# One transfer and one buffer for each 512 KB unit of weights in a decoder-layer kernel

## The chip, the cores and the metric

The kernel runs on one core of a Trainium2 chip. Its time is the device time of one launch in microseconds (us). TensorE (PE in the profile) does the matmuls, VectorE (DVE), ScalarE (ACT) and GpSimd (POOL) the rest, and SyncE (SP) issues nearly all transfers (DMAs) in the order of the program. Each of these engines works through its own list in order and waits at semaphores for the others. Sixteen DMA engines move the data.

## What is computed

One decoder layer in float32, for one sequence of 256 positions and 1024 channels. The reference, cut to its course:

```python
proj = x @ w_in                      # -> q | k | v | B | C | h | gate_attn | gate_conv
q, k = apply_partial_rope(q, cos, sin), apply_partial_rope(k, cos, sin)
y_att = moba_attention(q, k, v) @ w_attn_out
y_cnv = (gate_b * causal_dwconv(gate_c * h_in, conv_w_mix)) @ w_conv_out
mix = (g_att * y_att + g_cnv * y_cnv) @ w_o
x = layer_norm(DEEPNORM_ALPHA * x + mix, ln1_g, ln1_b)
u = causal_dwconv(x @ w_up, conv_w_ffn)
f = (silu(u[..., :D_FF]) * u[..., D_FF:]) @ w_down
x = layer_norm(DEEPNORM_ALPHA * x + f, ln2_g, ln2_b)
```

With 256 positions there is a single key block, so the attention is plain causal attention with 8 heads of 64. The feed-forward width is 2816.

## The kernel before

Every matmul is done with float32 operands that are split into a high part (cast to float32r) and a low part (the rest), and three products high x high, high x low and low x high are summed. So each weight that arrives must be split first: ACT casts the raw tile to the high part `wh` (lines 198 and 220), DVE subtracts it from the raw tile and gives the low part `wl` (lines 203 and 221). A *unit* is a piece of weights with 1024 float32 numbers in each of the 128 partitions, 512 KB. Six or twelve matmuls use it, and there are nine buffers for `wh` and nine for `wl`.

The host packs all weights into one array `wpack` in the order of their use, so a transfer is one contiguous read. `plan()` (line 73) lists the units and groups them in *chunks*. A chunk is one buffer and, with the exceptions in `PIECES` (line 52), one transfer. Most chunks hold two units: 2048 numbers, 8 KB in each partition, 1 MB. The first eight chunks hold one k-tile each of the product with q and k: 256 columns of the transposed x and one unit of weights, 5 KB in each partition. Chunk 0 is cut in three transfers and chunk 1 in two. `RAW_BUFS = 3` buffers of 8 KB take the chunks in turn.

`issue_dma(c)` (line 177) issues all chunks up to c on SP's queue. A transfer into a buffer that is still being read waits on SP until the split of the buffer's last unit is done, and SP's later transfers wait behind it. `split_start(u)` and `split_h(u)` (lines 189 and 194) call it for the chunk two after that of unit u, so a chunk's transfer is issued when the first unit of the chunk two before it is split.

The stages, in order of time:

- *q and k* (lines 595 to 618): for each of eight k-tiles, x's tile and the unit are split, and 12 matmuls of 512 columns follow. The splits of the first four v units stand among the last two k-tiles. After the last matmuls of q and of k, ACT evacuates them (`evac_rows`, line 556).
- *v, h, C, B and the gates* (lines 744 to 760): 16 units of 12 matmuls and 16 units of 16 matmuls. After each unit a *slot* (`mid_slot`, `step`, lines 527 and 740) emits the attention's and the convolution's tasks whose lag in slots is over, and `mid_ahead` (line 732) emits splits four to six units ahead of PE. Tasks that issue transfers are emitted before the slot's splits. Such are the exchanges that transpose through memory: rotated q and k are turned in blocks by DVE and written (`qk_write`, `qkd`), and three slots after that of the second write read back (`qk_read`, `qkl`); `qk_high` and `qk_low` then split them for the scores. The probabilities (`pd`, `sm`) and the convolution (`cvd`, `convl`) take the same way.
- *y, o and the first norm* (lines 786 to 856).
- *the feed-forward* (lines 968 to 1078): u and its convolution, with the exchange `ud`, `uts` through memory, the gated product and the down product; `slot(k)` splits four to seven units ahead of PE.

The pool `tmp` has six scratch buffers with the tag "scr", 2 KB in each partition, that hold small intermediate results in turn; in the q and k stage they are not in use.

Of the kernel before, what the change touches and what calls it, by code (L numbers as in the profile page):

```python
# [8 lines left out]
F32 = mybir.dt.float32  # L9
# [6 lines left out]
P = 128  # L16
S = 256
# [29 lines left out]
    return parts  # L47


CHUNK = 2048  # L50

PIECES = {0: (0, 256, 768, 1280), 1: (0, 768, 1280)}
OFF_V, OFF_B, OFF_C, OFF_H, OFF_G = 2 * AW, 3 * AW, 3 * AW + CW, 3 * AW + 2 * CW, 3 * AW + 3 * CW
TAIL = 8
GROUPS = NP // 2
# [17 lines left out]
def plan():  # L73


    chunks, units, first = [], [], {}

    def chunk(*us):
        c, off = len(chunks), 0
        chunks.append([])  # L80
        for k, n, blocks in us:
            chunks[c].append(len(units))
            units.append((c, off, k, n, blocks))
            off += k * n
        assert off <= CHUNK

    def mark(name):
        first[name] = len(units)

    def cols(w, c0):  # L90
        chunk(*[(8, P, [(w, 0, 8, c0 + u * P, c0 + (u + 1) * P)]) for u in range(2)])

    def rows(w, k):
        chunk(*[(1, D, [(w, k + u, k + u + 1, 0, D)]) for u in range(2)])


    mark("qk")
    for k in range(KT):
        chunk((1, S, [("xT", k, k + 1, 0, S)]), (2, 512, [("w_in", k, k + 1, 0, 1024)]))

    def wide(w, c0):
        for half in range(2):
            chunk(*[(2, 512, [(w, k, k + 2, c0, c0 + 512)]) for k in (4 * half, 4 * half + 2)])

    for off in (OFF_V, OFF_H, OFF_C, OFF_B):
        mark(off)
        wide("w_in", off)
    for pr in range(8):
        mark(("g", pr))
        cols("w_in", OFF_G + pr * 256)  # L110

    for half in range(2):
        for nm in ("ao", "co"):
            mark((nm, half))
            chunk(*[(4, 256, [(nm, 0, 4, half * 512 + u * 256, half * 512 + u * 256 + 256)]) for u in range(2)])
    mark("wo")
    for k in range(0, 8, 2):
        rows("w_o", k)

    for kind, c in [("u", 0)] + FFN_ORDER:  # L120
        mark((kind, c))
        if kind == "d":
            rows("w_dn", 2 * c)
            continue
        for half in range(2):
            chunk(*[(2, 512, [("w_up", k, k + 1, c0, c0 + 256)
                              for k in (4 * half + 2 * u, 4 * half + 2 * u + 1)
                              for c0 in (256 * c, DFF + 256 * c)]) for u in range(2)])
    return chunks, units, first
# [17 lines left out]
def layer_kernel(ctx: ExitStack, tc: tile.TileContext, x, wpack, cpack, ln1_g, ln1_b, ln2_g, ln2_b, out):  # L147
# [4 lines left out]
    wp = ctx.enter_context(tc.tile_pool(name="wp", bufs=1))  # L152
# [12 lines left out]
    def scratch(shape, name, bufs=None, tag="scr"):  # L165
        return tmp.tile(shape, F32, tag=tag, name=name, bufs=bufs or 6)

    RAW_BUFS, HL_BUFS, PR_BUFS = 3, 9, 4  # L170
    TURN = nc.sync
    chunks, plan_units, U = plan()
    blocks = transfers(chunks, plan_units)
    units = [dict(chunk=c, off=off, shape=(k, n), h=None, l=None) for c, off, k, n, _ in plan_units]
    raws = []

    def issue_dma(c):
        while len(raws) <= c and len(raws) < len(chunks):
            i = len(raws)
            t = wp.tile([P, CHUNK], F32, tag="raw", name=f"raw{i}", bufs=RAW_BUFS)  # L180
            raws.append(t)
            for a, b, off in blocks[i]:
                nc.sync.dma_start(t[:, a:b], wpack[off:off + P * (b - a)].rearrange("(p n) -> p n", p=P))

    def alloc(u, part, tag):
        k, n = units[u]["shape"]
        units[u][part] = wp.tile([P, k, n], F32R, tag=tag, name=f"{tag}{u}", bufs=HL_BUFS)

    def split_start(u):
        issue_dma(units[u]["chunk"] + RAW_BUFS - 1)  # L190
        alloc(u, "h", "wh")
        alloc(u, "l", "wl")

    def split_h(u):

        issue_dma(units[u]["chunk"] + RAW_BUFS - 1)
        alloc(u, "h", "wh")
        nc.scalar.activation(units[u]["h"], raw_of(u), AF.Copy)  # L198

# [19 lines left out]
    def hl_split(h, l, src, eng=None):  # L219
        nc.scalar.activation(h, src, AF.Copy)  # L220
        (eng or nc.vector).tensor_tensor(l, src, h.bitcast(F32), op=ALU.subtract)  # L221
# [5 lines left out]
    nc.gpsimd.memset(ident, 0.0)  # L227
    nc.gpsimd.affine_select(out=ident, in_=ident, compare_op=ALU.not_equal, fill=1.0, base=0,
                            pattern=[[-1, P]], channel_multiplier=1)
    issue_dma(1)  # L230
    warm = ps_bank("warm")

    def warm_up(n):
# [27 lines left out]
    xh, xl = xT[:, :, 0], xT[:, :, 1]  # L261
# [306 lines left out]


    def x_split(k):  # L570
        issue_dma(k + RAW_BUFS - 1)
        hl_split(xh[:, k, :], xl[:, k, :], raws[k][:, 0:S])

    def qk_split(k):
        if k < KT:
# [17 lines left out]


    split_start(1)
    issue_dma(RAW_BUFS - 1)
    nc.vector.tensor_copy(xh[:, 0, :], raws[0][:, 0:S])
    nc.vector.tensor_tensor(xl[:, 0, :], raws[0][:, 0:S], xh[:, 0, :].bitcast(F32), op=ALU.subtract)
    w0, wh0, wl0 = raw_of(1), units[1]["h"], units[1]["l"]
# [145 lines left out]
    for nm, off in (("v", OFF_V), ("h", OFF_H), ("c", OFF_C), ("b", OFF_B)):  # L745
        GB[nm] = [(ps_bank if nm == "v" else acc_bank)(f"{nm}{t}") for t in range(2)]
        for c in range(4):
            u = U[off] + c
# [4 lines left out]
    for j in range(16):  # L753
        u = U[("g", 0)] + j
# [6 lines left out]
    k = U[("ao", 0)] - C0  # L761
# [24 lines left out]
    for half in range(2):  # L786
        for e in range(2):
            ua, uc = U[("ao", half)] + e, U[("co", half)] + e
            for n in range(2):
                i = half * 4 + e * 2 + n  # L790
# [237 lines left out]
    for k, (kind, i, u) in enumerate(seq[:tail_from]):  # L1028
        if kind == "u":
            c, h = i  # L1030
# [56 lines left out]
def packed(inputs):  # L1087
# [6 lines left out]
    chunks, units, _ = plan()  # L1094
    rows = np.zeros((len(chunks), P, CHUNK), np.float32)
    for c, off, k, n, blocks in units:
# [27 lines left out]
```

## Time and profile before

| | us |
|---|---|
| three runs | 360.8, 361.29, 365.44 |
| median | 361.29 |
| profiled execution | 361.71 |
| its span (first to last instruction) | 359.9 |

Busy time in the span:

| engine | us | share |
|---|---|---|
| PE, matmuls | 348.8 | 97% |
| DVE | 298.3 | 83% |
| ACT | 208.5 | 58% |
| POOL | 64.6 | 18% |

The core moved 88.50 MB at 246 GB/s on average.

In the rows below, L with a number is the line of the kernel. A row of the timeline has the start of an instruction in us, its length, the engine, the line, the operation, the tile that it writes and, after the arrow, the tiles that it reads, then its size and how many like it were merged; in brackets stands how long the engine was idle just before, and what ended that. A row of the waits has who waited for whom, then us in total, times and the longest. `raw` is a chunk's buffer, `wpack` the packed weights, `wh` and `wl` a unit's parts, `xT` x's parts. Successive matmuls overlap, so a matmul's length is longer than the step from one to the next.

### The profile page before, as it was taken

The numbers are of one execution on the slowest core, as the hardware profiler recorded it, in microseconds if no ns is written. First come the engines' busy times: TensorE is split into PE (matmuls) and PEld (weight loads), VectorE is DVE, ScalarE is ACT, GpSimd is POOL, SyncE is SP. The second block draws the span as 40 slices with busy tenths as digits, with TensorE's granted clock in tenths as the row PEclk, the third lists the DMA queues.
The fourth block names the chain that finished last, engine by engine and source line by source line (L and its number), as shares of the span: only waits on it lengthen the run. The fifth ranks groups of instructions, "written<-read, shape, count | busy, mean of one in ns | idle before, by whom it ended". The sixth has DMA issues, their size and how long they took to land.

```text
span 359.9 us, 5040 instructions
## 1 busy us (share of the span) xinstructions
PE 348.8 (97%) x1762; PEld 294.5 (82%) x1762; DVE 298.3 (83%) x466; ACT 208.5 (58%) x346; POOL 64.6 (18%) x75
## 2 busy tenths in 40 slices
PE   8999999999999989999999999999999999999991
PEld 7787888888888979988888888888888888888891
DVE  4757939987899879869894999999899988798884
ACT  3659519769888955633362567756556745457200
POOL 2000000454442000102100221231130230230211
PEclk9999999999999999999999999999999999999997
DMA  7797788689995765496249999699969879856011
GB/s 255 274 308 279 295 229 300 227 291 322 273 320 171 300 237 201 180 345 239 112 176 335 280 298 312 233 291 334 305 224 294 289 232 323 252 192 188 0 60 58
DMA packets 33322, 88.50 MB, mean 246 GB/s; under 512 B 2704, under 2 KB 19472, under 8 KB 26000
## 3 DMA queue, kind: packets, MB, share of 16 engines
q1 hardware_dynamic: 32576, 85.88, 71.4%
q0 software_dynamic: 576, 2.10, 1.8%
q8 instruction: 14, 0.23, 0.3%
q10 hardware_dynamic: 144, 0.20, 0.2%
q14 instruction: 12, 0.10, 0.1%
HBM read 77.68 MB, written 10.49 MB: 245 GB/s over the span
## 4 chain that ended last, share of the span: by engine, by line
PE 83%; DMA 5%; DVE 5%; ACT 4%; issue 2%; POOL 1%; SPq 0%; DVEq 0%; ACTq 0%
PE up L309 11%; PE up L307 11%; PE up L308 11%; PE d L309 5%; PE d L308 5%; PE d L307 5%; DMA raw<-in_wpack 5%; PE g L336 5%; PE g L338 2%; PE o L309 2%; PE o L308 2%; PE o L307 2%; PE y L327 2%; PE y L328 2%; PE y L326 2%
## 5 line engine op out<-in xcount | busy, mean ns | idle before, releaser
L203 DVE TENSOR_TENSOR wl<-raw,wh 128x1024 fp32r<-128x1024 f32 x90 | 111.6, 1253 | 5.2 <-ACT wh L198 5.0
L198 ACT ACTIVATE wh<-raw 128x1024 fp32r<-128x1024 f32 x90 | 93.0, 1050 | 15.2 <-DMA raw<-in_wpack 14.7
L307 PE MATMUL up<-wh,x1T 128*128 128x512 f32 x176 | 68.6, 390 | 0.0
L309 PE MATMUL up<-wh,x1T 128*128 128x512 f32 x176 | 68.5, 389 | 0.0
L308 PE MATMUL up<-wl,x1T 128*128 128x512 f32 x176 | 68.5, 389 | 0.0
L923 POOL TENSOR_TENSOR ff<-fs,fc 128x256 f32<-128x256 f32 x22 | 30.3, 1378 | 131.3 <-DVE fc L914 128.5
L221 DVE TENSOR_TENSOR wl<-raw,wh 128x1024 fp32r<-128x1024 f32 (+1 forms) x34 | 37.9, 1141 | 7.8 <-ACT wh L220 7.6
L220 ACT ACTIVATE wh<-raw 128x1024 fp32r<-128x1024 f32 (+1 forms) x34 | 32.5, 987 | 13.0 <-DMA raw<-in_wpack 8.7
L309 PEld LDWEIGHTS up<-wh,x1T 128*128 128x128 f32 x176 | 33.0, 188 | 6.9
L308 PEld LDWEIGHTS up<-wl,x1T 128*128 128x128 f32 x176 | 33.0, 188 | 6.9
L307 PEld LDWEIGHTS up<-wh,x1T 128*128 128x128 f32 x176 | 33.0, 188 | 6.7
L336 PE MATMUL g<-xT,wh 128*128 128x512 f32 x128 | 32.0, 392 | 0.0
L926 ACT ACTIVATE f<-ff 128x256 fp32r<-128x256 f32 x22 | 9.2, 420 | 38.3 <-POOL ff L923 38.3
L307 PE MATMUL d<-wh,f 128*128 128x512 f32 x80 | 31.1, 389 | 0.0
L308 PE MATMUL d<-wl,f 128*128 128x512 f32 x80 | 31.1, 389 | 0.0
L309 PE MATMUL d<-wh,f 128*128 128x512 f32 x80 | 31.1, 389 | 0.0
L456 POOL TENSOR_SCALAR sm<-sm,st 128x128 f32<-128x128 f32 (+1 forms) x16 | 17.5, 1107 | 74.3 <-ACT wh L198 65.6
L912 DVE SCALAR_TENSOR_TENSOR second<-uts,consts,tap 128x256 f32<-128x256 f32 x44 | 23.7, 539 | 6.6 <-ACT tap L905 4.7
L905 ACT ACTIVATE tap<-uts,consts 128x256 f32<-128x256 f32 x44 | 20.3, 500 | 14.6 <-DMA uts<-ud 14.2
L336 PEld LDWEIGHTS g<-xT,wh 128*128 128x128 f32 x128 | 23.1, 188 | 4.3
L914 DVE SCALAR_TENSOR_TENSOR fc<-uts,consts,second 128x256 f32<-128x256 f32 x44 | 23.4, 533 | 1.6
L362 DVE STREAM_TRANSPOSE stg<-up 128x512 f32<-128x512 f32 x22 | 14.5, 695 | 8.8 <-PE up L309 8.8
(180 smaller groups left out, 632.9 us busy)
## 6 DMA issues: line engine op xcount, KB each, us to landing
raw<-in_wpack SPq DMA_DIRECT2D x57, 1024.0 KB, 6.1
ud<-stg SPq DMA_DIRECT2D x11, 512.0 KB, 4.0
uts<-ud SPq DMA_DIRECT2D x44, 128.0 KB, 5.5
raw<-in_wpack SPq DMA_DIRECT2D x6, 640.0 KB, 4.9
pd<-ps SPq DMA_DIRECT2D x4, 384.0 KB, 5.8
sm<-pd SPq DMA_DIRECT2D x16, 96.0 KB, 4.4
qkd<-qks SPq DMA_DIRECT2D x2, 512.0 KB, 3.4
qkl<-qkd SPq DMA_DIRECT2D x4, 256.0 KB, 4.6
```

The source lines that it names most:

```text
L198: nc.scalar.activation(units[u]["h"], raw_of(u), AF.Copy)
L203: nc.vector.tensor_tensor(units[u]["l"], raw_of(u), units[u]["h"].bitcast(F32), op=ALU.subtract)
L220: nc.scalar.activation(h, src, AF.Copy)
L221: (eng or nc.vector).tensor_tensor(l, src, h.bitcast(F32), op=ALU.subtract)
L307: nc.tensor.matmul(o, ah, bh, start=start, stop=False)
L308: nc.tensor.matmul(o, ah, bl, start=False, stop=False)
L309: nc.tensor.matmul(o, al, bh, start=False, stop=stop)
L336: nc.tensor.matmul(bank, un["h"][:, k, :], b[:, k].rearrange("p a s -> p (a s)"), start=k == 0, stop=False)
L905: nc.scalar.activation(rows_of(taps[i % 2][:, a, 1:S + 1]), unit_of(i, a), AF.Copy, scale=w_ffn(0, j))
L912: nc.vector.scalar_tensor_tensor(rows_of(sec[:, 1:S + 1]), unit_of(i, a), w_ffn(1, j), rows_of(first[:, 0:S]), op0=ALU.mult, op1=ALU.add)
L914: nc.vector.scalar_tensor_tensor(rows_of(FF["c", i][:, a]), unit_of(i, a), w_ffn(2, j), rows_of(sec[:, 0:S]), op0=ALU.mult, op1=ALU.add)
L923: nc.gpsimd.tensor_tensor(FF["f", i], FF.pop(("s", i)), FF.pop(("c", i))[:, 1], op=ALU.mult)
```

## The change

A chunk holds one unit. `CHUNK` goes from 2048 to 1024 numbers in each partition and `RAW_BUFS` from 3 to 6, so that the buffers have 24 KB in each partition as before, and each unit has a transfer of 512 KB with rows of 4 KB. The eight k-tiles of x become chunks of their own (128 KB, rows of 1 KB) and land in the scratch buffers "scr" in place of the raw buffers; unit 2k is x's k-tile k and unit 2k + 1 the weights that go with it. The first two weight units are cut in two transfers each.

`order_for(u)` replaces the direct call of `issue_dma`: it issues up to unit u + 5; while q and k are loaded, where every second unit is one of x, up to unit u + 10, at most 15, the last of that stage. The first call issues four units (two k-tiles) in place of two chunks (the same data), and the split of unit 1 then issues up to unit 11, the sixth k-tile.

```diff
-CHUNK = 2048
-
-PIECES = {0: (0, 256, 768, 1280), 1: (0, 768, 1280)}
+CHUNK = 1024
+
+PIECES = {1: (0, 512, 1024), 3: (0, 512, 1024)}
...
     def chunk(*us):
-        c, off = len(chunks), 0
-        chunks.append([])
         for k, n, blocks in us:
-            chunks[c].append(len(units))
-            units.append((c, off, k, n, blocks))
-            off += k * n
-        assert off <= CHUNK
+            assert k * n in (S, CHUNK)
+            chunks.append([len(units)])
+            units.append((len(units), 0, k, n, blocks))
...
-    RAW_BUFS, HL_BUFS, PR_BUFS = 3, 9, 4
+    RAW_BUFS, HL_BUFS, PR_BUFS = 6, 9, 4
...
             i = len(raws)
-            t = wp.tile([P, CHUNK], F32, tag="raw", name=f"raw{i}", bufs=RAW_BUFS)
+            if i < U[OFF_V] and i % 2 == 0:
+                t = scratch([P, S], f"x{i // 2}")
+            else:
+                t = wp.tile([P, CHUNK], F32, tag="raw", name=f"raw{i}", bufs=RAW_BUFS)
...
+    def order_for(u):
+
+        c = u + RAW_BUFS - 1
+        issue_dma(max(c, min(2 * c - u, U[OFF_V] - 1)) if u < U[OFF_V] else c)
...
     def split_start(u):
-        issue_dma(units[u]["chunk"] + RAW_BUFS - 1)
+        order_for(u)
...
     def split_h(u):
 
-        issue_dma(units[u]["chunk"] + RAW_BUFS - 1)
+        order_for(u)
...
-    issue_dma(1)
+    issue_dma(3)
...
     def x_split(k):
-        issue_dma(k + RAW_BUFS - 1)
-        hl_split(xh[:, k, :], xl[:, k, :], raws[k][:, 0:S])
+        hl_split(xh[:, k, :], xl[:, k, :], raws[2 * k])
...
     split_start(1)
-    issue_dma(RAW_BUFS - 1)
+    issue_dma(5)
```

## The prediction

> **What bounds the kernel now.** I read the slices of the page first, then the busy time by stretch, then TensorE's (PE's) timeline for the places where it does not go on at once.
>
> ```profile
> PE   8999999999999989999999999999999999999991
> DMA  7797788689995765496249999699969879856011
> ```
>
> PE is at nine tenths nearly everywhere; the 16 DMA engines are often at five to eight. The windows give the same by stage (columns: length, then busy time of PE, weight load, DVE, ACT, POOL, then granted clock, DMA share, GB/s).
>
> ```profile
> 0.00:9.00 9.00, 7.80 (x50) 6.36 (x51) 4.36 (x9) 3.38 (x5) 1.99 (x21) 1.00 0.80 255
> ...
> 4.50:28.00 23.50, 22.81 (x99) 17.83 (x98) 15.17 (x34) 13.51 (x21) 0.00 (x0) 1.00 0.86 305
> ...
> 56.00:102.00 46.00, 46.00 (x270) 39.36 (x271) 39.46 (x83) 37.18 (x75) 19.83 (x18) 1.00 0.86 271
> 102.00:128.00 26.00, 24.46 (x146) 21.48 (x145) 22.97 (x38) 23.66 (x50) 6.12 (x7) 1.00 0.76 283
> 128.00:150.00 22.00, 21.92 (x177) 21.64 (x177) 19.63 (x32) 12.48 (x18) 0.87 (x2) 1.00 0.48 168
> ...
> 182.00:352.00 170.00, 170.00 (x774) 141.73 (x772) 147.82 (x209) 91.04 (x147) 31.31 (x23) 1.00 0.76 244
> ```
>
> From 182 us to 352 us PE is busy for all 170.00 us: earlier weights can win nothing there. What is left is in the gaps of the first 128 us. The timeline of PE shows them (start, length, then idle time and its releaser in brackets).
>
> ```profile
> 7.64 0.50 PE L591 MATMUL q<-wh,xT 128*128 128x512 f32 x1
> 8.36 0.50 PE L591 MATMUL q<-wl,xT 128*128 128x512 f32 x1 [0.22 <-DVE wl L221]
> ...
> 13.70 0.39 PE L591 MATMUL q<-wh,xT 128*128 128x512 f32 x1
> 14.55 0.50 PE L591 MATMUL q<-wl,xT 128*128 128x512 f32 x1 [0.46 <-DVE wl L221]
> ...
> 28.08 0.39 PE L307 MATMUL v<-wh,xT 128*128 128x512 f32 x1
> 28.68 0.50 PE L308 MATMUL v<-wl,xT 128*128 128x512 f32 x1 [0.21 <-DVE wl L221]
> ...
> 29.25 0.40 PE L307 MATMUL v<-wh,xT 128*128 128x512 f32 x1
> 29.48 0.39 PE L308 MATMUL v<-wl,xT 128*128 128x512 f32 x1
> ...
> 125.58 0.28 PE L326 MATMUL y<-aT,wh 128*128 128x256 f32 x1
> 125.70 0.33 PE L327 MATMUL y<-aT,wh 128*128 128x256 f32 x1
> 125.87 0.27 PE L328 MATMUL y<-aT,wl 128*128 128x256 f32 x1
> 127.68 0.38 PE L326 MATMUL y<-aT,wh 128*128 128x256 f32 x1 [1.54 <-ACT aT L515]
> 128.15 0.39 PE L327 MATMUL y<-aT,wh 128*128 128x256 f32 x1
> ```
>
> Unhindered, a 512-column matmul starts 29.48 - 29.25 = 0.23 us after the one before it, a 256-column one 125.70 - 125.58 = 0.12 us. Against that step PE loses 8.36 - 7.64 - 0.23 = 0.49 us, 14.55 - 13.70 - 0.23 = 0.62 us and 28.68 - 28.08 - 0.23 = 0.37 us: 1.48 us in the stage that loads x and the q, k and first v weights. At the end of the attention it loses 127.68 - 125.87 - 0.12 = 1.69 us and 128.15 - 127.68 - 0.12 = 0.35 us, together 2.04 us. These five gaps, 3.52 us, are about all that any change to loading can win: 1% of the time.
>
> **The change part by part.**
>
> Transfers. A unit of 512 KB feeds 12 matmuls of 512 columns, 12 x 0.23 = 2.7 us, so PE consumes 524 KB / 2.7 us = 193 GB/s. The buffers hold 24 KB per partition before and after. What changes is that a unit can be split when its own 512 KB are there, and that a freed unit gives its buffer back at once.
>
> ```profile
> raw<-in_wpack SPq DMA_DIRECT2D x57, 1024.0 KB, 6.1
> ud<-stg SPq DMA_DIRECT2D x11, 512.0 KB, 4.0
> ...
> L183 SPq DMA_DIRECT2D raw<-in_wpack x68: 327/336/437, 0.7 to 324.7; - x68
> ```
>
> These are issues of the DMA view (count, size, median us to landing) and the row of line 183. With one buffer in splitting, two transfers are in flight before: 2 x 1.05 MB / 6.1 us = 344 GB/s. After it are five: even at the old landing time 5 x 0.52 MB / 6.1 us = 430 GB/s, more than the engines move. So the number in flight does not get short.
>
> Rows of 4 KB instead of 8 KB: the trace has none in this queue, so I bound it. Rate over share is 305 / 0.86 = 355 GB/s in the window 4.5:28, mostly 5 KB rows, and 168 / 0.48 = 350 GB/s in 128:150, 8 KB rows: no price. In 0:9, with 1 to 5 KB rows, it is 255 / 0.80 = 319 GB/s: 10% longer. Ends: none and 10%; I take none, as 5 KB is nearest. Even 10% on the raw part of 182:352 (193 of its 244 GB/s) lifts its share from 0.76 to 0.82: hidden behind PE.
>
> A rule speaks against the change. The Trainium skill, "DMA: Bandwidth & Descriptors", section "Bandwidth", says to batch transfers to at least 1 MiB for three quarters of peak; its section "Anatomy of one DMA" has a fit of 2.0 us plus bytes over 436 GB/s. By that fit, as an estimate, 512 KB takes 3.2 us, and if transfers ran one behind the other 119 units would take 381 us. The trace disagrees with that reading: 640 KB and smaller transfers reach 355 GB/s at full share, since several are in flight.
>
> Issues. 68 become 132 (8 of x, 10 for the eight q/k units, 114 others): 64 x 0.336 = 21.5 us more on SP, spread over the span. SP also waits now at each unit rather than at every second.
>
> ```profile
> SPq L183 <- DVE wl L203: 57.7, 24, 7.7
> ...
> 195.31 1.06 ACT L198 ACTIVATE wh<-raw 128x1024 fp32r<-128x1024 f32 x1 [6.31 <-DMA raw<-in_wpack]
> ```
>
> SP stands 57.7 us in such waits, and behind it stand the writes and reads of the exchanges (qkd, pd, cvd, ud). After 128 us I cost this at nothing: the cover is the lookahead. The longest wait for a raw buffer, 6.31 us at 195.31, lies inside the 170.00 us in which PE never stops. Without that cover a late unit would cost PE its lateness.
>
> The start. x's tiles take scratch buffers, so six k-tiles are issued without a wait, where k-tile 3 waited for buffer 0.
>
> ```profile
> 6.53 5.32 DMA raw<-in_wpack
> ...
> 18.41 7.87 DMA raw<-in_wpack
> ...
> 6.64 0.42 ACT L220 ACTIVATE xT<-raw 128x256 fp32r<-128x256 f32 x1 [0.86 <-DMA raw<-in_wpack]
> ...
> 13.27 1.23 DVE L221 TENSOR_TENSOR wl<-raw,wh 128x1024 fp32r<-128x1024 f32 x1 [0.53 <-ACT wh L220]
> ...
> 18.50 0.42 ACT L220 ACTIVATE xT<-raw 128x256 fp32r<-128x256 f32 x1 [1.81 <-DMA raw<-in_wpack]
> ```
>
> The first two rows are of the chain that ended last: it runs through the landings of k-tile 3 (6.53 to 11.85) and of the first v chunk (18.41 to 26.28).
> - Gap of 0.49: x1 lands before its weights, so its cast, 0.42 us on ACT between landing and weight split, is done early. Ends 0 and 0.42; I take 0.35, since the next cast starts a little before one ends.
> - Gap of 0.62: PE waits for a split that ends 13.27 + 1.23 = 14.50. By 9 us 9 x 255 = 2.30 MB have moved; k-tile 3 is complete at 2.70 MB (four k-tiles and the constants), at 319 to 355 GB/s 1.1 to 1.3 us later, some 10.3 us, or 11 with a late engine. That is 0.9 to 1.5 us earlier: gain 0.62. It would be 0 if the landing stayed at 11.85.
> - Gap of 0.37: unit v0 is complete at 5.85 MB (eight k-tiles of 0.655 MB, the constants, 0.52 MB). (5.85 - 2.30) / 0.305 is 11.6 us after 9 us: 20.6 us. Before, by the same rate, 2.30 + 17.3 x 0.305 = 7.6 MB had moved by 26.28, when the 6.4 MB up to its chunk were complete; a landing comes 3 to 4 us later than the mean rate says, so I add 3 us: 23.6 against 26.28. Gain 0.37.
>
> Next late would be k-tile 7, whose cast stands behind k-tile 6 (landed 18.41) and the rotary table; k-tile 6 comes 1 us or more earlier too. Sum: 1.3 us, ends 0 and 1.48.
>
> The attention. The same late landing delays more than PE. On ACT the evacuations of q and k stand behind the v splits, and the turned q and k go through memory.
>
> ```profile
> 26.30 2.01 ACT L220 ACTIVATE wh<-raw 128x1024 fp32r<-128x1024 f32 x2 [2.45 <-DMA raw<-in_wpack]
> ...
> 31.74 1.09 ACT L558 ACTIVATE qk<-k 128x512 f32<-128x512 f32 x2
> ...
> 52.81 1.16 ACT L409 ACTIVATE qkT<-qkl 128x512 fp32r<-128x512 f32 x2 [7.65 <-DMA qkl<-qkd]
> ...
> 38.71 0.33 SPq L183 DMA_DIRECT2D raw<-in_wpack  x1
> 41.24 0.33 SPq L392 DMA_DIRECT2D qkd<-qks  x1
> 45.37 2.09 SPq L398 DMA_DIRECT2D qkl<-qkd  x4
> 47.56 0.87 SPq L183 DMA_DIRECT2D raw<-in_wpack  x2
> ...
> ACT sm L446 <- DVE st L439: 5.8, 2, 5.2
> ACT aT L515 <- POOL ac L512: 2.8, 3, 1.2
> ```
>
> ACT waits 7.65 us for qkl. The last two rows head ACT's waits from 54 us to 128 us: they are for DVE and POOL, not PE. In 102:128 ACT is busy 23.66 of 26.00 us and DVE 22.97. So from the landing of qkl on these two engines, not PE, set when the attention ends, and PE's 2.04 us of waiting is their lateness. If v0 lands 2.7 us earlier, so does the evacuation of k at 31.74, bounded by PE's own end of k, 1 us earlier. Against it, one 512 KB unit (1.5 us at 350 GB/s) now goes into the queue ahead of qkl's reads, where the issue at 47.56 stood behind them; but only half of the megabyte of 38.71 is left ahead of qkd. I take qkl 2.3 us earlier, 1.0 us more than PE's 1.3: the 2.04 us shrink by 1.0. Ends: 2.04, and a loss of all that the start won.
>
> Sum: 1.3 + 1.0 = 2.3 us. The profiled execution took 361.71 us (span 359.9), 0.4 us above the median of 361.29: 361.71 - 2.3 = 359.4, and by the median 359.0.
>
> **The rivals.**
>
> *The start's gain is eaten.* ACT and DVE arrive at 127.68 as before because qkl does not move, so PE comes earlier and waits longer. For it: their waits above hold no PE. Against it: the evacuation waits for the landing that moves. The same time results if early issue does nothing, as the engines' share in 4.5:28 is 0.86 already; but that leaves 0.14 x 23.5 = 3.3 us. Time: 361.3, or 360.0 where only the attention's part fails.
>
> *Slower: the new waits on SP.* Unit 28's issue stands before qkl's reads and waits for DVE; if qkl lands later than 52.81, each us is one at 127.68. With the 1.5 us above and no help from v0: 361.3 + 1.5 = 362.8. It decides by over 2% only if qkl came 7 us late, 60 us.
>
> *Slower: small transfers.* If the 4 KB rows cost so much that the share of 182:352 reaches 1.00, the raw part (0.79 of 0.76, 0.60) would be 0.84, 1.4 times as long; from there on PE waits. At 1.5 times the share is 1.06, 170 x 0.06 = 10 us: 371. The rows at 319 GB/s speak against it. The rule of the Trainium skill, "DMA: Bandwidth & Descriptors", section "Bandwidth", points this way; no row here bears it out.
>
> **How the numbers follow.** The forecast (both parts win something) has 0.60, the eaten gain 0.27, SP's waits 0.09, small transfers 0.04. Predicted is the first: 359.0. The low end takes all five gaps, 361.3 - 3.5 = 357.8, and 0.8 for gaps that I didn't count: 357.0. The high end takes in the eaten gain with half a microsecond of spread: 361.8. What is left out above is 0.13, below 0.05. About 2%, 7.2 us, is what a measurement of this kernel can tell from no change. Faster by that would need twice the gaps: 0.01. Slower needs the last rival or a very late qkl: 0.03. Within 2%: 0.96.
>
> **What would show it.** The start: PE's gaps at 8.4, 14.5 and 28.7 us are gone, and the first full unit after the q/k weights lands near 23 us. The attention: qkl's first use before 51 us, and PE's wait for aT near 126 us below 1.1 us. The transfers: DMA share in the 170 us of the feed-forward between 0.74 and 0.83, and PE busy all through. I am wrong if the wait for aT grows, if qkl lands after 52.8, or if PE waits for wl anywhere after 130 us.

## The result, and the profile after

| | runs | median us | lowest to highest us |
|---|---|---|---|
| before, on the same chip | 20 | 363.51 | 360.17 to 366.06 |
| changed | 20 | 359.75 | 358.97 to 360.90 |

The ratio is 0.991 with a 95% interval of 0.9886 to 0.9935. That is within 2%, and clear of the spread: 0.009 x 363.5 = 3.3 us (the two medians in the table are 3.8 us apart). The predicted 359.0 (range 357.0 to 361.8) holds the time. The two profiled executions differ by half of that: 361.71 before (span 359.9), 360.12 after (span 358.3), 1.6 us. The lowest runs differ by 1.2 us. So two things have to be explained: where 1.6 us come from in the profile, and why before's runs spread over 5.9 us and the changed kernel's over 1.9 us.

First the slices of the changed kernel's page, then its busy time by stretch, with the columns that the prediction names.

```profile
PE   8999999999999999999999999999999999999991
DMA  8989897789996866687168999899889989992011
```

```profile
0.00:9.00 9.00, 8.02 (x53) 7.30 (x54) 4.70 (x10) 3.86 (x6) 1.99 (x21) 1.00 0.84 245
...
4.50:28.00 23.50, 22.79 (x100) 18.34 (x99) 17.86 (x36) 16.79 (x25) 0.00 (x0) 1.00 0.94 342
...
126.00:148.00 22.00, 21.77 (x175) 21.43 (x176) 19.55 (x30) 12.93 (x19) 0.42 (x1) 1.00 0.58 187
180.00:350.00 170.00, 170.00 (x772) 141.63 (x771) 148.43 (x209) 91.72 (x147) 31.35 (x23) 1.00 0.80 245
```

In the feed-forward's 170 us PE stays busy, at a DMA share of 0.80 where it was 0.76. From 4.5 us to 28 us the engines move 342 GB/s in place of 305: the transfers do start earlier. What PE makes of it stands in its timeline; ahead of its rows stand SP's issue of the weights of k-tile 2 and ACT's first cast of them.

```profile
4.48 0.43 SPq L183 DMA_DIRECT2D raw<-in_wpack  x1
...
10.13 1.15 ACT L225 ACTIVATE wh<-raw 128x512 fp32r<-128x512 f32 x2 [2.38 <-DMA raw<-in_wpack]
...
9.94 0.39 PE L595 MATMUL k<-wh,xT 128*128 128x512 f32 x1
10.81 0.50 PE L595 MATMUL q<-wh,xT 128*128 128x512 f32 x1 [0.48 <-ACT wh L225]
11.54 0.50 PE L595 MATMUL q<-wl,xT 128*128 128x512 f32 x1 [0.23 <-DVE wl L226]
...
38.66 0.39 PE L312 MATMUL h<-wh,xT 128*128 128x512 f32 x1
...
124.82 0.28 PE L333 MATMUL y<-aT,wl 128*128 128x256 f32 x1
126.15 0.38 PE L331 MATMUL y<-aT,wh 128*128 128x256 f32 x1 [1.06 <-ACT aT L520]
126.61 0.39 PE L332 MATMUL y<-aT,wh 128*128 128x256 f32 x1
```

The gaps at 7.6, 13.7 and 28.1 us are gone, and two new ones are there: 10.81 - 9.94 - 0.23 = 0.64 us and 11.54 - 10.81 - 0.23 = 0.50 us, for the weights of k-tile 2. These are issued at 4.48 us, behind eight other transfers, and cast at 10.13 us, 5.65 us later. Before, the chunk of k-tile 2 was issued at 3.53 us, behind six, and its x was cast at 9.28 us, 5.75 us later. So the issue is late, not the landing after it. PE's wait near 126 us is 1.33 - 0.12 = 1.21 us and 0.46 - 0.12 = 0.34 us, together 1.55 us in place of 2.04 us. PE comes to it 125.87 - 124.82 = 1.05 us earlier than before. It ends at 126.15 us where it ended at 127.68 us: 1.53 of the 1.6 us are won ahead of this point. From it to the span's end the profile before has 232.22 us, the one after 232.15 us.

Where the 1.53 us are won shows on ACT, which casts the weights and evacuates q and k.

```profile
21.87 3.89 ACT L225 ACTIVATE wh<-raw 128x1024 fp32r<-128x1024 f32 x4
25.94 1.28 ACT L563 ACTIVATE qk<-q 128x512 f32<-128x512 f32 x2 [0.18 <-PE q L595]
...
28.06 1.08 ACT L563 ACTIVATE qk<-k 128x512 f32<-128x512 f32 x2
...
49.81 1.16 ACT L414 ACTIVATE qkT<-qkl 128x512 fp32r<-128x512 f32 x2 [8.45 <-DMA qkl<-qkd]
```

Before, ACT waited 2.45 us for the first v units and cast them at 26.30 us. Now they are three of the four casts that follow each other from 21.87 us on, and no landing holds ACT up. The evacuation of k comes 31.74 - 28.06 = 3.68 us earlier. Next in line is DVE: the split that follows, the rotation and the turn. These are its rows, before (the first two) and after.

```profile
33.81 1.23 DVE L203 TENSOR_TENSOR wl<-raw,wh 128x1024 fp32r<-128x1024 f32 x1 [0.70 <-ACT wh L198]
39.91 1.30 DVE L362 STREAM_TRANSPOSE qks<-qk 128x512 f32<-128x512 f32 x2
```

```profile
30.12 1.23 DVE L208 TENSOR_TENSOR wl<-raw,wh 128x1024 fp32r<-128x1024 f32 x1 [0.69 <-ACT wh L203]
36.23 1.30 DVE L367 STREAM_TRANSPOSE qks<-qk 128x512 f32<-128x512 f32 x2
```

The whole chain moves by 3.68 us, and SP's queue with it.

```profile
37.56 0.33 SPq L397 DMA_DIRECT2D qkd<-qks  x1
38.67 0.33 SPq L183 DMA_DIRECT2D raw<-in_wpack  x1
40.84 1.81 SPq L403 DMA_DIRECT2D qkl<-qkd  x4
42.70 2.07 SPq L183 DMA_DIRECT2D raw<-in_wpack  x4
```

The second write of `qkd` is issued 41.24 - 37.56 = 3.68 us earlier. The last of the four reads was issued at 45.37 + 2.09 = 47.46 us and is at 40.84 + 1.81 = 42.65 us: 4.8 us earlier. But their data are used only 3.00 us earlier: from the last read's issue to the first use it took 52.81 - 47.46 = 5.35 us and takes 49.81 - 42.65 = 7.16 us.

### The profile page after: what moved, and what is told of

It is laid out like the page before. It is cut to its first block, busy times and chain, and to the rows that moved or that the text cites. A ratio compares the mean times of both kernels' runs of the same rounds, so it can differ in the third digit from the quotient of the medians.

```text
span 358.3 us, 5242 instructions
## 1 busy us (share of the span) xinstructions
PE 347.9 (97%) x1762; PEld 294.8 (82%) x1762; DVE 298.0 (83%) x466; ACT 208.6 (58%) x346; POOL 64.6 (18%) x75
## 4 chain that ended last, share of the span: by engine, by line
PE 67%; DMA 9%; DVE 7%; ACT 7%; issue 4%; POOL 4%; SPq 1%; DVEq 0%; ACTq 0%; POOLq 0%
PE up L312 11%; PE up L314 11%; PE up L313 11%; PE d L314 5%; PE d L312 5%; PE d L313 5%; DMA sm<-pd 3%; DMA raw<-in_wpack 3%; POOL sm L461 3%; ACT wh L203 2%; PE q L595 2%; DMA qkl<-qkd 2%; PE o L313 2%; PE o L312 2%; PE o L314 2%
```

## The experiments

Two theories stood against each other. One: the gain comes through `qkl`, by the earlier landing of the first v units. The other: it comes from the start, or from the small transfers later on. A third question was what makes before's runs spread. This table has one profiled execution of each kernel, and three of the kernel before: the first matmul of the h stage on PE, SP's issue of the second write of `qkd`, ACT's first use of `qkl`, the end of PE's wait for `aT` (in brackets its idle time), and from there to the end of the span.

| | us | h | qkd | qkl | wait's end | rest |
|---|---|---|---|---|---|---|
| before | 361.71 | 39.47 | 41.24 | 52.81 | 127.68 (1.54) | 232.2 |
| before_again | 363.42 | 39.23 | 40.05 | 52.31 | 127.80 (1.53) | 233.7 |
| before_third | 363.60 | 38.70 | 41.14 | 52.80 | 128.09 (1.53) | 233.7 |
| before_fill | 361.44 | 38.36 | 39.24 | 51.95 | 127.43 (0.41) | 232.3 |
| before_evac | 366.64 | 38.54 | 40.23 | 54.48 | 130.77 (1.53) | 234.1 |
| changed | 360.12 | 38.66 | 37.56 | 49.81 | 126.15 (1.06) | 232.2 |
| start_only | 359.65 | 38.67 | 37.65 | 49.92 | 125.66 (0.55) | 232.2 |
| depth3 | 359.71 | 38.70 | 37.59 | 49.80 | 125.73 (0.59) | 232.2 |
| x_act | 360.64 | 39.30 | 38.20 | 49.44 | 126.65 (0.91) | 232.2 |
| after_order | 360.33 | 38.19 | 37.67 | 50.97 | 126.38 (1.53) | 232.1 |
| after_late | 360.13 | 38.73 | 37.63 | 50.42 | 126.16 (0.99) | 232.1 |
| after_hold | 360.30 | 38.97 | 37.86 | 48.80 | 126.31 (0.91) | 232.2 |
| late_wait | 361.65 | 38.44 | 37.34 | 50.63 | 127.34 (2.46) | 232.2 |
| late_busy | 361.48 | 38.58 | 37.48 | 50.65 | 127.14 (0.32) | 232.3 |

**The kernel before once more** (before_again, without an edit).

> The kernel before, looked at once more, since its runs lie between 360.2 us and 366.1 us and those of the changed kernel between 359.0 us and 360.9 us. My theory: what makes it longer in some executions is a late landing in the q and k stage (k-tiles 3 to 7 or the first v chunk), which comes back at the end of the attention as a longer wait of PE for aT. In an execution of 363 us or more, PE's gaps before 30 us and the wait near 126 us together are over 5 us (3.5 us in the profile shown). Rival: the extra time lies after 130 us, in waits of PE for wl in the feed-forward. In an execution of about 361 us the gaps are as shown and nothing is told apart.

It took 363.42 us. The 1.7 us more than in the first profile stand in neither of the expected places: up to the wait's end the two differ by 0.12 us, and 1.5 us lie in the rest. The windows of one microsecond behind the wait show them in before_again; the second fence is the first profile of before.

```profile
128.00:129.00 1.00, 0.92 (x7) 0.74 (x7) 0.20 (x1) 1.00 (x2) 0.00 (x0) 1.00 0.98 393
129.00:130.00 1.00, 1.00 (x8) 1.00 (x7) 0.87 (x1) 1.00 (x3) 0.00 (x0) 0.61 0.26 107
130.00:131.00 1.00, 1.00 (x7) 1.00 (x6) 1.00 (x2) 0.99 (x2) 0.00 (x0) 0.50 0.00 0
...
132.00:133.00 1.00, 1.00 (x8) 1.00 (x8) 0.96 (x3) 0.42 (x1) 0.00 (x0) 0.69 0.52 66
```

```profile
130.00:131.00 1.00, 1.00 (x10) 1.00 (x9) 1.00 (x2) 0.88 (x1) 0.00 (x0) 1.00 0.00 0
```

The granted clock (the third number from the end) falls to 0.50 soon after PE's wait. PE is "busy" for the whole microsecond in both, but starts 7 matmuls in place of 10. In the same stretch successive 256-column matmuls of before_again start 0.22 us apart, in place of 0.12 us:

```profile
130.03 0.41 PE L326 MATMUL y<-yT,wh 128*128 128x256 f32 x1
130.25 0.41 PE L327 MATMUL y<-yT,wh 128*128 128x256 f32 x1
```

**Only the q and k stage changed** (start_only): x and its weights as in the change, later chunks of 1 MB in three buffers of 8 KB as before.

```diff
-CHUNK = 1024
+CHUNK = 2048
...
-    RAW_BUFS, HL_BUFS, PR_BUFS = 6, 9, 4
+    RAW_BUFS, HL_BUFS, PR_BUFS = 3, 9, 4
...
+            elif i < U[OFF_V] and i % 4 == 3:
+                t = whole[0][:, CHUNK // 2:CHUNK]
             else:
-                t = wp.tile([P, CHUNK], F32, tag="raw", name=f"raw{i}", bufs=RAW_BUFS)
+                whole[0] = t = wp.tile([P, CHUNK], F32, tag="raw", name=f"raw{i}", bufs=RAW_BUFS)
...
-        c = u + RAW_BUFS - 1
-        issue_dma(max(c, min(2 * c - u, U[OFF_V] - 1)) if u < U[OFF_V] else c)
+        c = u + 5
+        last = max(c, min(2 * c - u, U[OFF_V] - 1))
+        issue_dma(min(last, units[last]["chunk"]) if u < U[OFF_V] else units[u]["chunk"] + RAW_BUFS - 1)
```

> The changed kernel's q and k stage (x in scratch, six k-tiles issued at the start), but from v on two units in one transfer of 1 MB and one buffer of 8 KB, three of these, as before. My theory (the start and the earlier landing of v give the gain, the size of later transfers nothing): ratio to before 0.989 to 0.995, qkl first used by ACT before 51 us, PE's wait for aT near 126 us 1.0 to 1.6 us. Rival (the gain comes from units that land and free their buffers by themselves): ratio 0.997 to 1.002.

Median 360.36 us, ratio 0.9933 (0.9898 to 0.9968), `qkl` at 49.92 us. PE's wait, 0.55 us, is shorter than expected. The interval holds the change's ratio: the later small transfers add nothing that shows.

**The small transfers with shallow loading at the start** (depth3): of the six buffers every second is to be passed over while q and k are loaded, so that three k-tiles are ahead as before.

```diff
+                if i < U[OFF_V]:
+                    wp.tile([P, CHUNK], F32, tag="raw", name=f"skip{i}", bufs=RAW_BUFS)
                 t = wp.tile([P, CHUNK], F32, tag="raw", name=f"raw{i}", bufs=RAW_BUFS)
...
-        c = u + RAW_BUFS - 1
-        issue_dma(max(c, min(2 * c - u, U[OFF_V] - 1)) if u < U[OFF_V] else c)
+        issue_dma(u + 4 if u < U[OFF_V] else u + RAW_BUFS - 1)
```

> The changed kernel with one thing undone: in the q and k stage only every second of the six buffers is used, so that k-tile k's weights wait until k-tile k-3 is split, as before the change. Units keep their own transfers and buffers, x stays in scratch. My theory: the gaps of PE near 14.5 us and 28 us come back (0.4 to 0.7 us each), qkl is first used after 51 us, ratio to before 0.995 to 1.001. Rival (units by themselves give the gain): ratio 0.989 to 0.994, as with the change.

Median 359.88 us, ratio 0.9919 (0.9889 to 0.9948), `qkl` at 49.80 us: the expected gaps did not come back, and nothing was lost. But the edit held nothing back. SP issues the weights of k-tiles 4 and 5 at 6.39 and 7.84 us and the first v unit at 12.28 us; in the change it does so at 6.38, 7.63 and 12.24 us, and before the change the chunks of k-tiles 4 and 5 went out at 8.94 and 11.57 us and the first v chunk at 18.41 us. So this run repeats the change and says nothing on the depth. What start_only, depth3 and the change have in common is that x has transfers and buffers of its own, that the transfers are issued this early, and that the first v units are there when ACT comes to them: the four casts without a wait begin at 21.98, 21.93 and 21.87 us.

**x from another queue** (x_act): the new gap at 9.94 us could be SP's time to issue 16 transfers, so five of x's go out from ACT's queue.

```diff
-                nc.sync.dma_start(t[:, a:b], wpack[off:off + P * (b - a)].rearrange("(p n) -> p n", p=P))
+                queue = nc.scalar if i in (2, 4, 6, 8, 10) else nc.sync
+                queue.dma_start(t[:, a:b], wpack[off:off + P * (b - a)].rearrange("(p n) -> p n", p=P))
```

> The changed kernel, but x's k-tiles 1 to 5 are issued from ACT's queue, which is idle then, so that SP issues the weights of k-tile 2 some 0.9 us sooner. In the changed kernel PE loses 0.64 us and 0.50 us at 10 us to 11.5 us, as these weights land near 10.1 us. If SP's issue time makes them late: they land at 9.2 us or so, both gaps are under 0.2 us, and the ratio to before is about 0.002 to 0.004 below the 0.991 of the change. If the DMA engines are what is full (share 0.84 in the first 9 us): landing and gaps stay within 0.3 us and the ratio is that of the change.

Median 360.59 us, ratio 0.994 (0.9913 to 0.9968). The weights of k-tile 2 are cast at 10.26 us, against 10.13 us in the change. But the edit did not make SP issue them earlier: in this profile SP waits for the landing of x ahead of the weights of k-tile 1 (issued at 3.39 us in place of 2.58 us), and issues those of k-tile 2 at 4.93 us, in the change at 4.48 us. So the run doesn't show whether SP or the engines hold them up; the next one does.

**The order at the start** (after_order): k-tile 2 ahead of the constants, and k evacuated before the split of the fourth v unit.

```diff
     consts = cst.tile([P, 162], F32, name="consts")
+    issue_dma(5)
     nc.sync.dma_start(consts, cpack)
...
-            if k >= KT - 2:
+            if k == KT - 2 or (k == KT - 1 and m == 0):
                 split(C0 + 2 * (k - KT + 2) + m)
...
+        if k == KT - 1:
+            split(C0 + 3)
```

> The changed kernel with two moves: k-tile 2 is issued ahead of the 81 KB of constants, and k is evacuated ahead of the split of the fourth v unit. The gap of PE near 10.8 us (0.64 us) shrinks to 0.2 to 0.4 us, as k-tile 2's weights land 0.3 us earlier; evacuation of k moves 0.3 us. If both count, ratio to before 0.988 to 0.990, 0.5 to 0.8 us under the change. If the landing does not move (the engines interleave the transfers): ratio 0.991.

Median 360.74 us, ratio 0.9946 (0.9921 to 0.9971). The weights of k-tile 2 are issued 0.48 us earlier than in the change, at 4.00 us, and cast 0.79 us earlier, at 9.34 us, and PE's gaps near 10.8 us are gone. Earlier issue does bring an earlier landing here. This kernel has the earliest h of all, and gains nothing by it:

```profile
38.19 0.39 PE L313 MATMUL h<-wh,xT 128*128 128x512 f32 x1
...
50.97 1.15 ACT L415 ACTIVATE qkT<-qkl 128x512 fp32r<-128x512 f32 x2 [10.09 <-DMA qkl<-qkd]
...
126.38 0.38 PE L332 MATMUL y<-aT,wh 128*128 128x256 f32 x1 [1.53 <-ACT aT L521]
```

h begins 0.47 us earlier than in the change, but `qkl` is used 1.16 us later, PE waits 0.47 us longer, and the wait ends 0.23 us later. k is evacuated at 26.83 us, 1.23 us earlier than in the change, and yet the second write of `qkd` goes out 0.11 us later.

**k evacuated earlier, with the transfers of before** (before_evac): if the order on ACT were the cause, this would be the gain without the change.

```diff
-            if k >= KT - 2:
-                split(C0 + 2 * (k - KT + 2) + m)
+            if k == KT - 2:
+                split(C0 + m)
...
+        if k == KT - 1:
+            split(C0 + 2)
+            split(C0 + 3)
```

> The kernel before with its transfers unchanged: only the splits of the third and fourth v unit stand behind the evacuations of q and k on ACT, not ahead of them. Theory (the part of the change that counts beyond PE's early gaps is that q and k are evacuated earlier): k is evacuated by 30.5 us instead of 32.8, qkl is first used 1.5 to 2.5 us earlier than 52.8 us, PE's wait near 126 us shrinks from 2.0 us to 1.0 to 1.5 us, the clock does not fall, and the runs lie together near 360.3 us: ratio 0.990 to 0.995. Rival (the transfers' own effect): ratio 0.998 to 1.002.

Median 363.31 us, ratio 1.0008 (0.9979 to 1.0036): nothing. Its profiled execution is the slowest of its 12 runs, so its places are read here and not its time.

```profile
27.18 1.28 ACT L558 ACTIVATE qk<-k 128x512 f32<-128x512 f32 x2
28.35 2.00 ACT L220 ACTIVATE wh<-raw 128x1024 fp32r<-128x1024 f32 x2
31.69 2.01 ACT L198 ACTIVATE wh<-raw 128x1024 fp32r<-128x1024 f32 x2 [1.35 <-DMA raw<-in_wpack]
```

The evacuation of k comes at 27.18 us, even earlier than in the change, but the rotation on DVE stands behind the split of the next unit, whose megabyte ACT awaits until 31.69 us. The second write of `qkd` is issued at 40.23 us, 1.0 us earlier than before, but the reads of `qkl` begin at 46.92 us in place of 45.37 us. So the order on ACT alone wins nothing: the landing of the next units sets the rotation's time, and with the old chunks these land late.

**qkl's reads first** (after_hold): units from the 13th after q and k on are not issued before the reads of `qkl`, to remove the price that the reads paid in the queue.

```diff
     def issue_dma(c):
+        if "qkl" not in TN:
+            c = min(c, U[OFF_V] + 11)
```

> The changed kernel, but units from the 13th after q and k on are not issued before the reads of qkl. In the changed kernel qkl's use comes 7.2 us after the last of its reads is issued, before the change 5.4 us. If the raw units ahead of the reads on the queue are the cause (the prediction's price of 1.5 us for the slower case): use of qkl 1.0 to 1.8 us earlier, at 48.0 to 48.8 us, and PE's wait near 126 us shorter by up to 0.5 us, as ACT then waits for PE more; ratio 0.989 to 0.991. If other traffic is the cause: qkl within 0.5 us of 49.8 us, ratio 0.991.

Median 359.60 us (8 runs), ratio 0.9916 (0.9883 to 0.9949): level with the change. In the change a 512 KB unit goes out at 38.67 us, between the last write of `qkd` and the reads; here it does not, and from the last read's issue (41.20 + 1.81 = 43.01 us) to the first use of `qkl` it takes 5.79 us in place of 7.16 us. `qkl` comes 1.0 us earlier, and the wait's end doesn't move:

```profile
41.20 1.81 SPq L404 DMA_DIRECT2D qkl<-qkd  x4
...
48.80 1.15 ACT L415 ACTIVATE qkT<-qkl 128x512 fp32r<-128x512 f32 x2 [7.14 <-DMA qkl<-qkd]
...
126.31 0.38 PE L333 MATMUL y<-aT,wh 128*128 128x256 f32 x1 [0.91 <-ACT aT L521]
```

Why, a row of the changed kernel's ACT shows: it no longer has work to bring forward everywhere, but waits for PE. In after_hold this wait is 3.30 us long and ends at 78.25 us, 0.30 us later than in the change, as h began 0.31 us later.

```profile
77.95 0.39 ACT L681 ACTIVATE gs<-g 128x256 f32<-128x256 f32 x1 [1.99 <-PE g L343]
```

**The spread of before's runs.** Four kernels and a third profile of before bear on it. In before_fill, 20 matmuls of zeros stand in PE's queue ahead of those that wait for `aT`; the transfers are those of before.

```diff
+            if fill is not None and k == nk - 1:
+                for _ in range(20):
+                    nc.tensor.matmul(fill[:, 0:P], zeros, zeros, start=True, stop=True)
```

> The kernel before with nothing changed in its transfers: 20 matmuls of zeros (128 x 128, bf16, into an unused bank, some 1.2 us in all) stand before the matmuls of y that wait for the last aT near 126 us, so that PE is not idle there. Theory of the clock: in the second look at the kernel before, the granted clock fell to 0.50 from 129.2 us to 132.5 us, just after PE's wait of 1.5 us, which cost some 1.6 us; in the first look it did not fall. If such falls are what most runs of the kernel before pay, this kernel has none: its runs lie within 2 us of each other, median 361.2 us, ratio 0.993 to 0.997. Rival (the spread of the runs before comes from transfers): median and spread as before, ratio 0.998 to 1.002.

Median 362.30 us (361.15 to 365.31), ratio 1.0002 (0.9972 to 1.0033). The expectation is missed. PE's idle time is 0.41 us in place of 1.54 us, and the runs spread all the same. The profiled execution shows the filling:

```profile
125.73 1.29 PE L327 MATMUL fill<-zeros 128*128 128x128 bf16 x20
127.43 0.39 PE L329 MATMUL y<-aT,wh 128*128 128x256 f32 x1 [0.41 <-ACT aT L518]
```

after_late was meant to lengthen the changed kernel's wait, by two casts on ACT.

```diff
     def attend_high(p):
+        if p == 3:
+            late = scratch([P, 384], "late")
+            for _ in range(2):
+                nc.scalar.activation(late, mask, AF.Copy)
```

> The changed kernel with two casts of 384 columns (0.5 us each) on ACT ahead of the last cast to aT, so that PE's wait near 126 us is 1.0 us longer, some 2.5 us with what follows it. Theory of the clock: the wait costs its 1.0 us in each run, and a fall of the granted clock to 0.50 for 3.4 us comes back in most runs: median 361.5 to 363 us, runs 3 us or more apart. Rival (the clock doesn't follow the wait's length): median 360.8 us, runs within 2 us of each other as with the change.

Median 360.23 us (359.66 to 362.16), ratio 0.9931 (0.9905 to 0.9957). The casts lay in time in which ACT waited for POOL, PE's wait stayed at 0.99 us, and the run told nothing on the question. late_wait has three casts that read POOL's sum, so that they stand behind ACT's wait for it and ahead of the cast that PE waits for; late_busy has the same casts and 32 matmuls of zeros in PE's wait.

```diff
     def attend_high(p):
+        if p == 3:
+            late = scratch([P, S], "late")
+            for _ in range(3):
+                nc.scalar.activation(late, PR[p, "c"][:, 0], AF.Copy)
```

> The changed kernel with three casts of 256 columns (0.42 us each) between GpSimd's last sum and the last cast to aT, all reading that sum, so that none of them hides in ACT's wait for it, as the two casts of the run before (after_late) did. PE's wait near 126 us grows from 1.1 us to some 2.3 us. Theory of the clock (a long wait lets the granted clock fall for 3.4 us in some or most executions): median 361.6 to 363.2 us, runs 2.5 us or more apart, and where the profile shows the fall, the time from the wait's end to the last instruction is 1.5 to 2 us over the usual 232.2 us. Rival: only the wait itself counts, median 361.0 us, runs within 2 us.

> The same with 32 matmuls of zeros (128 x 128, bf16, into an unused bank, some 1.9 us) ahead of the matmuls that wait, so that PE is busy for most of the wait. Theory of the clock: the wait costs its 1.2 us and nothing else, median 361.0 us, runs within 2 us, no fall. Rival (what spreads the runs is not PE's idle time): as late_wait, whatever that is.

late_wait: median 362.06 us (360.82 to 365.34), ratio 0.9984 (0.9953 to 1.0016). late_busy: median 361.54 us (360.57 to 362.24), ratio 0.9964 (0.9938 to 0.999). The runs of the one spread over 4.5 us, of the other over 1.7 us, so idle PE time seems to matter; the medians' difference, 0.5 us, is not clear of the intervals. But in its profiled execution late_wait waits 2.46 us, and the clock holds:

```profile
127.34 0.39 PE L331 MATMUL y<-aT,wh 128*128 128x256 f32 x1 [2.46 <-ACT aT L524]
```

```profile
130.00:131.00 1.00, 1.00 (x11) 1.00 (x10) 1.00 (x2) 0.53 (x1) 0.00 (x0) 1.00 0.10 37
```

The last is a third profile of the unedited kernel before (before_third).

> A third look at the kernel before. Its time is to be the sum of three parts: when PE's wait for aT ends (127.7 us and 127.8 us in the first two looks), 232.2 us from there to the last instruction, and 1.5 to 2 us more where the granted clock fell after that wait. If qkl is used later than 53 us the first part is later by about as much.

It took 363.60 us, and its clock falls in the same place:

```profile
116.75 0.50 PE L496 MATMUL av<-vpt 128*128 128x512 f32 x1 [0.94 <-DVE vpt L487]
128.09 0.39 PE L326 MATMUL y<-aT,wh 128*128 128x256 f32 x1 [1.53 <-ACT aT L515]
```

```profile
130.00:131.00 1.00, 1.00 (x6) 1.00 (x6) 1.00 (x2) 1.00 (x2) 0.00 (x0) 0.50 0.00 0
```

All three profiles with a fall (before_again, before_third, before_evac) also have a wait of 0.28 to 0.94 us about 11 us earlier, at 116 to 119 us, and the first profile of before and that of the change don't. before_fill has one of 0.77 us and no fall, with its later wait filled.

A closer reading, by windows of 0.1 us, makes more of this. The three falls begin at 129.21 us (before_again), 129.88 us (before_third) and 132.49 us (before_evac), and each lasts 3.41 us. After PE's last matmul the clock falls once more, in all three 228.69 us after the first fall: 67 steps of 3.413 us. So in each execution the clock seems to change only on a grid of 3.41 us, which lies elsewhere in each. In the other profiles the grid can be counted back from their fall at the end. PE's wait for `aT` then lies on it so:

| | PE idle, us | its parts in the steps of the grid, us | fall after it |
|---|---|---|---|
| before_again, before_third, before_evac | 1.53 | 1.53 | yes |
| late_wait | 2.46 | 1.42 and 1.04 | no |
| before | 1.54 | 1.25 and 0.29 | no |
| after_order | 1.53 | 0.57 and 0.96 | no |
| the eight others | 0.32 to 1.06 | 0.32 to 1.06 | no |

All fourteen fit one rule: the clock is halved for the next step when PE idled 1.53 us or more within one step, and is not at 1.42 us or less. The falls at the end fit it too: in all fourteen the step ahead of the fall has 2.00 us or more without matmuls, and the step ahead of that 1.32 us or less. The earlier waits at 116 to 119 us are not needed for it. The rule was found in these profiles afterwards; no run was made to test it.

The runs without a profile have their mean granted clock on record, and it tells the falls apart: 0.990 or 0.991 in the three profiles with a fall (half of 3.41 us in 361 us is 0.005), 0.992 to 0.996 in the others. Of 87 runs of the kernel before that were timed beside these experiments 38 lie at 0.991 or below, with a median of 364.0 us, and 49 above, with 362.1 us. Of the changed kernel's 20 runs none lies that low, of late_busy's 12 none, of late_wait's 12 six, and of before_fill's 12 two, where the kernel before beside it has 18 of 33. The other kernels with x in transfers of its own have some too: after_order, with a wait of 1.53 us in its profile, 4 of 12, after_late 2 of 10, start_only and depth3 one of 12 each, x_act and after_hold none. So fewer runs fall where PE's wait is filled, in both kernels. before_fill's runs spread all the same, as those of before without a fall do, from 360.45 to 366.55 us: the falls are not the only cause of the spread.

## Why the prediction was right or wrong

- **Bound.** Right. After the wait's end every kernel without a fall of the clock takes 232.1 to 232.3 us, with 4 KB rows or 8 KB rows, and in the feed-forward PE is busy without a break.
- **The start, 1.3 us.** Wrong as a term. All three gaps went, and the two new ones, 1.14 us, gave most of it back: h began 39.47 - 38.66 = 0.81 us earlier, and PE came to its wait 1.05 us earlier. The step that failed is the cost of the issues, "64 x 0.336 = 21.5 us more on SP, spread over the span", which the start was not charged for. There SP issues without a pause, one transfer in about 0.47 us, and two more of them ahead of the weights of k-tile 2 made these 0.95 us late. The rows of 1 to 4 KB are not what made them late, as the landing took no longer after the issue (5.65 against 5.75 us). Rate over share in the first 9 us, 245 / 0.84 = 292 GB/s where it was 319, differs as much between kernels with the same transfers there: it is 248 / 0.75 = 331 in late_busy. The gain is also not one of the change alone: before_fill, before_evac and before_third have the transfers of before and begin h at 38.36 to 38.70 us. And by itself it is worth nothing: in before_third h came as early as in the changed kernel, `qkl` at 52.80 us, and the wait ended at 128.09 us. For this part the rival "the start's gain is eaten" describes what happens; after_order shows it on the changed kernel.
- **The attention, 1.0 us.** Right in its mechanism, with its sizes off. `qkl` was to come 2.3 us earlier, and came 3.00 us earlier. The evacuation of k was taken as bound to PE's end of k, 1 us earlier; it moved by 3.68 us, as it had stood behind the v casts all along. The queue price for `qkl`'s reads was estimated at 1.5 us; 7.16 - 5.35 = 1.8 us were paid, of which after_hold gave back 7.16 - 5.79 = 1.4 us. Of the 3.00 us, only 1.53 us arrive at the wait's end, and the wait shrinks by 2.04 - 1.55 = 0.49 us, not by 1.0. The prediction had ACT and DVE set the end from the landing of `qkl` on. With `qkl` before 50 us this no longer holds: after_hold's further 1.0 us brought nothing, and ACT waits 1.99 us for PE at 77.95 us.
- **The sum.** 1.3 + 1.0 = 2.3 us were forecast; the profiles have 1.05 + 0.49 = 1.54 us of it, each term too large, and 361.29 - 1.54 is the 359.75 us that were measured. That the measured ratio gives a gain of the forecast's order, 3.3 us, is luck: it is taken against 20 runs of before with a median of 363.51 us, which a further effect (below) makes longer than the three runs that the forecast went out from. How much of the 1.53 us the start would bring alone is not settled. At the same start of h, before_third and the change differ by 128.09 - 126.15 = 1.94 us, so most comes through `qkl`. But once `qkl` is early the start counts: in x_act h begins 0.64 us later than in the change, ACT's wait for PE ends 0.64 us later, and PE's wait for `aT` 0.50 us later. These are single profiles; start_only's wait ends 0.49 us ahead of the change's with h and `qkl` as there.
- **The other rivals.** SP waits more often for splits in the second part, and the time in it grows little, by rows of the changed kernel's waits and issues:

```profile
SPq L183 <- DVE wl L208: 64.7, 47, 7.2
...
raw<-in_wpack SPq DMA_DIRECT2D x120, 512.0 KB, 5.0
```

  They were 57.7 us in 24 waits. The exchange came earlier in spite of them, and after the wait's end they cost nothing. Small transfers: from 180 us to 350 us rate over share is 245 / 0.80 = 306 GB/s. start_only, with 1 MB in that stage, has 244 GB/s at a share of 0.76: 321. That is 5%, inside the ends of none and 10%, and hidden as forecast. (The prediction's 119 units are 122, 8 with q and k and 114 behind them; nothing hangs on it.) The rule of the Trainium skill, "DMA: Bandwidth & Descriptors", section "Bandwidth", to batch to 1 MiB or more, thus has 5% on its side in the engines' time, and nothing in the kernel's.
- **What the prediction didn't have at all** is the second part of the measured gain. The ratio gives 3.3 us, the profiles 1.6 us. Three of five profiles of kernels with before's transfers show the fall of the clock, worth 233.7 - 232.2 = 1.5 us; none of nine of kernels with x in transfers of its own does. By their mean clock 38 of 87 runs of before have such a fall, worth 364.0 - 362.1 = 1.9 us in the median, and none of the changed kernel's 20. By the rule read from the grid this follows from the shorter wait: 1.54 us can lie whole within one step, and does so in some executions, while 1.06 us stays below 1.42 us wherever it lies. As a rough sum, 38 / 87 of 1.9 us is 0.8 us; with the profiles' 1.6 us that is 2.4 of the 3.3 us.
- **Still open:** the remaining 0.9 us, and why runs of before without a fall still spread over 6 us; before_evac's profile, with its wait's end at 130.77 us, shows that the wait itself can come 3 us late with the transfers of before. Also open is which part of the start's edit counts, the separate x or the early issue, as no run has one without the other. And the rule of the clock wants a run of its own.

## What to carry to other kernels

When several engines hand work on, ask what stands in line behind a late landing, not only what idles at it: here 2.45 us of waiting on ACT moved a chain through DVE, SP and memory by 3.7 us, while the visible gaps on PE were worth nothing as long as that chain was late. Let the next stage's first weights be issued before the current stage has given its buffers back; here that went with giving the small operand that is needed early (x) buffers of its own. Count the issues ahead of the first transfers, one by one; the size of later transfers hardly matters while a long cover hides them. Take more than one profile before pricing gaps of half a microsecond: three profiles of the same kernel began a stage between 38.70 and 39.47 us. And read the granted clock of all runs, not of the profiled one alone.

## What the runs showed of the hardware that was not expected

- The granted clock can fall to 0.50 for 3.41 us after a wait in which PE idled only 1.53 us; matmuls of 256 columns then start 0.22 us apart, and 1.5 us are lost. The Trainium skill, "TensorE: Matmul & The Clock Gate", section "What's actually happening", has the clock halved after an idle window of about 3.4 us, with windows that run freely. The half clock, its 3.41 us and windows that run freely agree with the traces: in three profiles the falls lie on a grid of 3.41 us, elsewhere in each. A window that is idle as a whole is not needed here: 1.53 us within one step were enough in three profiles, 1.42 us were not in another, and a wait of 2.46 us that lay across two steps was spared.
- Reads with a 512 KB transfer issued between them and the write they wait for were used 7.16 us after the last one's issue, and 5.79 us without it (after_hold).
- While SP issues without a pause, one issue follows another after about 0.47 us, and a later issue is a later landing: the weights of k-tile 2, issued at 4.00 us (after_order), 4.48 us (changed) and 4.93 us (x_act), were cast at 9.34, 10.13 and 10.26 us, 5.3 to 5.7 us after their issue.
